# Two-layer hybrid trunk: pair sums in PSUM, weight forms by accumulating DMAs, q, k and v stored in split form

## The chip, the cores and the metric

The kernel runs on one core of a Trainium2 chip. A core has five engines that each work through their own queue in order: TensorE (PE, matrix products into PSUM; its weight loads are shown apart as PEld), VectorE (DVE), ScalarE (ACT), GpSimd (POOL) and SyncE (SP), which here issues nearly all DMAs. The metric is the device time of the whole program in microseconds (us).

## The reference

Two layers, each on 1024 tokens of width 1024, float32:

```python
ada = c_act @ w_ada[l] + b_ada[l]
shift, scale, gate = jnp.split(ada, 3, axis=-1)
h = rmsnorm(x, norm_g[l]) * (1.0 + scale) + shift
p = h @ w_in[l]                       # 1024 x 9224
mq, mk, mv, mo, mz, mi, mf, rq, rk, rv, rz = split_cols(p)
qk = silu(causal_dwconv(concat([mq, mk]), conv_w[l], conv_b[l]))
cell = mlstm_chunkwise(mq_c, mk_c, mv, mi + b_igate[l], mf + b_fgate[l])      # 4 heads x 256
y_m = sigmoid(mo) * head_layernorm(cell, gn_m[l]) * silu(mz)
ret = retention_chunkwise(rotary(rq), rotary(rk), rv)                         # 4 heads x 256
y_r = head_layernorm(ret, gn_r[l]) * silu(rz)
x = x + gate * (concat([y_m, y_r]) @ w_out[l])
```

At the end stands one more RMSNorm. Both kinds of head are causal attention with decay, computed block by block with a running state of 256 x 256: a block's scores (q times k, masked and scaled), the values (scores times v, plus q times the state), and the update of the state (k scaled, times v).

## The kernel before

**Precision.** Each matrix operand is split into a high part of type float32r and a low part, the rest (split_to, L741: ACT writes the high part, POOL or DVE subtracts it from the source). A product is three matmuls (mm3, L149): high x high, high x low, low x high.

**Products in pairs.** The projection p is made by pairs of 128-column tiles (for v: pairs of heads). For two column tiles and two halves of the tokens, eight block products are replaced by seven on sums of blocks (Strassen's way). build_forms (L560) makes the sums of h once a layer; weight_forms (L589) makes those of the weights for every pair: four raw blocks of 128 x 512 come from HBM, four sums are formed in place (on POOL for q and k, on DVE for gates and v, L597 to L603), and seven splits follow (ACT and POOL). pair_units (L659) takes one weight form after the other, in the order of ORDER (L587), and issues 12 matmuls with it into one of the PSUM banks X, Y, Z; combine (L642) copies partial sums to SBUF tiles "acc" (ACT, L646) and adds the next bank to them (DVE, L649); done(...) gets a finished tile of 128 x 512, in SBUF but for the last one, which stays in its bank X. For v, vpair_units (L671) does the same with 48 matmuls of 256 columns per form, one set of banks from each of the PSUM pools pp and pa (four banks each). The Feeder (L629) makes weight forms four ahead (AHEAD); the tiles wH and wL have five buffers each (NW), raw has four.

**After a product.** A z or o tile goes through a gate (L532, L537) and is stored in DRAM (gdr). A q or k tile goes through a short convolution (conv_silu, L745) or a rotation (rot_done, L817), and spill (L795) stores it in DRAM as float32 (qdr, kfr), k also transposed (kdr, L762). v is stored as it is (vdr).

**Attention** of a head (L844) is a generator that is launched when its k is done. It is advanced between products: each unit of a pair is one tick, and "yield n" means that the next piece comes n ticks later. fetch_qk (L852) loads a block of q and k and splits it; fetch_kv (L862) loads v, scales and splits it (v_split, L722), and loads and splits the transposed k (k_rows, L770). A block takes four steps:

```python
for j in range(NCH):
    scores(j + 1); dm_load(j + 2); fetch_kv(j + 1)
    yield 1
    values(j, ...)            # whole blocks: and yield 1
    update(...)               # of the state; dm_make(j + 2)
    yield 1                   # divided blocks (j = 1, 2): values, update of their second half, yield 1
    fetch_qk(j + 2); finish(j)
    yield 1
```

**Order.** The order on PE is the program's own (manual schedule); those of ACT, DVE, POOL and SP are set by a scheduler, which also waits for free buffers. In a layer, v of all eight heads comes first, then for each head q, k and a pair of gates; then the output product (OutLoads L1074, out_units L1104). norm, gate_chain (L443) and rotary_tables (L383) stand around these.

Of the kernel before, what the change touches and what calls it, by code (L numbers as in the profile page):

```python
# [19 lines left out]
P = 128  # L20
# [16 lines left out]
NB = 60  # L37
NACC = 8
NTH = 4
NW = 5  # L40
AHEAD = 4
# [16 lines left out]
N_CONST = 17  # L58


def shape_constants():
    c = np.zeros((P, N_CONST), np.float32)
    step = np.arange(128, dtype=np.float32) * (np.float32(1.0) / np.float32(127.0))
    c[:, C_FREQ] = np.float32(1.0) / (10000.0 ** step.astype(np.float64)).astype(np.float32)
    p = np.arange(P, dtype=np.float64)
    for h in range(NH):
        for tt in range(2):
            c[:, C_GS + 2 * h + tt] = GAMMA[h] ** (-(p + 128 * tt))
            c[:, C_EPS + 2 * h + tt] = EPS * 256.0 * GAMMA[h] ** (-2.0 * (p + 128 * tt))
    return c  # L70
# [15 lines left out]
def tile_hybrid_trunk(ctx, tc, x, xt, c, positions, w_ada, b_ada, norm_g, w_in, conv_w, conv_b,  # L86
# [89 lines left out]
    qdr, kfr = ([[[dpool.tile([HD, HALF], F32, name=f"{n}{l}_{h}_{i}") for i in range(2)] for h in range(8)]  # L176
                 for l in range(DEPTH)] for n in ("qdr", "kfr"))
    vdr = [[[dpool.tile([HALF, HD], F32, name=f"vdr{l}_{h}_{i}") for i in range(2)] for h in range(8)]
           for l in range(DEPTH)]
    mdr = [dpool.tile([NH, T], F32, name=f"mdr{l}") for l in range(DEPTH)]  # L180

# [29 lines left out]
    def head_cols(l, rb):  # L211
# [4 lines left out]
        V.tensor_copy(cl[:, 8:88], pt[:, 0:80])  # L216
        V.tensor_scalar(cl[:, 88:96], pt[:, 80:88], 0.25, None, ALU.mult)
        V.tensor_scalar(cl[:, 96:104], pt[:, 88:96], 0.5, None, ALU.mult)
# [128 lines left out]
    def load_w_raw(src, c0, n):  # L347
        kk = 512 // n
        raws = []
        for p in range(KT // kk):  # L350
            raw = wt("raw", 512, 4)
            Q.dma_start(raw.rearrange("p (a b) -> p a b", a=kk),
                        src[p * kk * P:(p + 1) * kk * P, c0:c0 + n].rearrange("(a p) b -> p a b", p=P))
            raws.append(raw)
            yield raw

    def split_w(raw, n, eng=G, other=False):
        wH, wL = (wt(t, 512, b, F32R) for t, b in ((("acc", NACC),) * 2 if other else (("wH", NW), ("wL", NW))))
        split_to((wH, wL), raw, eng)
        return [(wH[:, a * n:(a + 1) * n], wL[:, a * n:(a + 1) * n]) for a in range(512 // n)]  # L360

    def load_w(src, c0, n):
        res = []
        for raw in load_w_raw(src, c0, n):
            res += split_w(raw, n)
        return res
# [16 lines left out]
    def rotary_tables():  # L383
# [5 lines left out]
        for n in range(4):  # L389
# [6 lines left out]
            yield 1  # L396
            V.tensor_tensor(a2, ang, a1, ALU.subtract)
            V.tensor_scalar(turn, a1, c3, None, ALU.mult)
            yield 1
            V.scalar_tensor_tensor(turn, a2, c3, turn, ALU.mult, ALU.add)  # L400
            V.scalar_tensor_tensor(turn, a2, c2, turn, ALU.mult, ALU.add)
            yield 1
# [17 lines left out]
            yield 2  # L420
# [22 lines left out]
    def gate_chain(l, pgs, gt):  # L443
# [6 lines left out]
        mxs = wt("q", 1024, 2)  # L450
        for half in range(2):
            pg = pgs[half]
            fb, li, e = wt("v", 516, 4)[:, 0:512], wt("v", 516, 4)[:, 0:512], wt("dm", 512, 2)
# [57 lines left out]
        eH, eL = wt("eH", 64, 1, F32R), wt("eL", 64, 1, F32R)  # L511
        A.copy(eH, eul)
        V.tensor_tensor(eL, eul, f(eH), ALU.subtract)
# [16 lines left out]
        gt.update(C4=C4, eul4=eul4, eH=eH, eL=eL, em3=em3, wi=wi, we=we, dc=dc)  # L530

    def gate_z(src, g):  # L532
        th = wt("th", 512, NTH)
        A.activation(th, src, AF.Tanh, scale=0.5)
        V.scalar_tensor_tensor(g, th, 1.0, src, ALU.add, ALU.mult)

    def gate_o(src, g, store):  # L537
        th = wt("th", 512, NTH)
        A.activation(th, src, AF.Tanh, scale=0.5)
# [20 lines left out]
    def build_forms(hT):  # L560
        F = {"11": [hT[k][0] for k in range(4)], "21": [hT[k][0] for k in range(4, 8)],
             "22": [hT[k][1] for k in range(4, 8)], "T1": [], "T2": [], "T3": [], "T4": []}
# [11 lines left out]
        for k in range(4):  # L574
            t1, b12, b22 = whole(hT[k][0]), whole(hT[k][1]), whole(hT[k + 4][1])
            V.tensor_tensor(t1, b12, t1, ALU.subtract)
            V.tensor_tensor(b12, b22, b12, ALU.subtract)
            V.tensor_tensor(b22, b22, t1, ALU.subtract)
            keep("T2", b22)
            keep("T1", t1)  # L580
            keep("T3", b12)
            t4 = whole(hT[k + 4][0])
            V.tensor_tensor(t4, t4, b22, ALU.subtract)
            keep("T4", t4)
        return F

    ORDER = (("X", "11"), ("Y", "21"), ("X", "T2"), ("Z", "T1"), ("X", "T3"), ("Z", "22"), ("X", "T4"))  # L587

    def weight_forms(r11, r12, r21, r22, eng):  # L589
        def split(r):  # L590
            w = (wt("wH", 512, NW, F32R), wt("wL", 512, NW, F32R))
            split_to(w, r)
            return w

        yield split(r11)
        yield split(r12)
        eng.tensor_tensor(r21, r21, r22, ALU.add)  # L597
        eng.tensor_tensor(r11, r21, r11, ALU.subtract)  # L598
        yield split(r11)
        yield split(r21)  # L600
        eng.tensor_tensor(r21, r22, r11, ALU.subtract)
        yield split(r21)
        eng.tensor_tensor(r12, r12, r11, ALU.subtract)  # L603
        yield split(r12)
        yield split(r22)

    def pair_forms(l, cols2, eng):
        raws = {}
        for i, kh in ((0, 0), (0, 1), (1, 0), (1, 1)):
            raw = raws[i, kh] = wt("raw", 512, 4)  # L610
            Q.dma_start(raw.rearrange("p (a b) -> p a b", a=4),
                        w_in[l, kh * 512:(kh + 1) * 512, cols2[i]:cols2[i] + P].rearrange("(a p) b -> p a b", p=P))
        for w in weight_forms(raws[0, 0], raws[0, 1], raws[1, 0], raws[1, 1], eng):
            yield [(w[0][:, k * P:(k + 1) * P], w[1][:, k * P:(k + 1) * P]) for k in range(4)]

    def vpair_forms(l, cols2, eng):
        gens = []
        for kp in range(2):
            raws = {}
            for i, kh in ((0, 0), (0, 1), (1, 0), (1, 1)):  # L620
                raw = raws[i, kh] = bt() if kp else wt("raw", 512, 4)
                r0 = kh * 512 + kp * 256
                Q.dma_start(raw.rearrange("p (a b) -> p a b", a=2),
                            w_in[l, r0:r0 + 256, cols2[i]:cols2[i] + HD].rearrange("(a p) b -> p a b", p=P))
            gens.append(weight_forms(raws[0, 0], raws[0, 1], raws[1, 0], raws[1, 1], eng))
# [16 lines left out]
    def combine(n, bank, keep, done):  # L642
        with tc.high_priority():
            if n in (0, 2, 3):
                keep[n] = wt("acc", 512, NACC)
                A.copy(keep[n], bank["Z" if n == 3 else "X"])  # L646
            elif n < 6:
                b, m = {1: ("Y", 0), 4: ("X", 3), 5: ("Z", 2)}[n]
                V.tensor_tensor(keep[m], bank[b], keep[m], ALU.add)  # L649
        if n == 1:  # L650
            done(0, 0, keep[0])
        elif n == 4:
            done(1, 1, keep[3])
        elif n == 5:
            done(0, 1, keep[2])
        elif n == 6:
            done(1, 0, bank["X"])

    def pair_units(feed, F, done):  # L659
        bank, keep = {}, {}  # L660
        for n, (b, form) in enumerate(ORDER):
# [6 lines left out]
            combine(n, bank, keep, done)  # L668
            yield

    def vpair_units(l, feed, F, heads):  # L671
        banks, keeps = [{}, {}], [{}, {}]

        def stored(part):
            def done(i, half, src):
                if i == 1 and half == 0:
                    t = wt("acc", 512, NACC)
                    A.copy(t, src)
# [844 lines left out]
```

## Time and profile before

| | |
|---|---|
| time, median of 3 runs | 2886.41 us (2884.13 to 2889.84) |
| the profiled execution | 2891.24 us, of which the span of the trace is 2889.5 us |
| mean granted clock of TensorE | 0.893 |
| bytes read from HBM, written | 251.90 MB, 105.94 MB |
| longest total wait on TensorE's queue, one line | 126.2 us (L896 for POOL's split of q) |

The profile gives each engine's busy time and, for groups of equal instructions, count, busy time, mean duration of one, the idle time of the engine before them and what ended it. Lines are those of the kernel printed above; since split_to and mm3 are helpers, many groups have the lines L742, L743 and L150 to L152, and are told apart by their tiles ("wL<-raw,wH" is the low part of a weight form, "q<-acc,q" that of a fetched q). Windows are counted from the start of the span. PEclk is the clock granted to TensorE as a share of the full one.

### The profile page before, as it was taken

Reading aid. Unit: us, or ns where it says so; the run is one execution under the profiler, and the core shown is the slowest. Engines: PE = TensorE matmul, PEld = TensorE weight load, DVE = VectorE, ACT = ScalarE, POOL = GpSimd, SP = SyncE. Lnnn points to the kernel's source line nnn. Section 1 sums busy time; section 2 is a strip of 40 time slices with the busy share of each in tenths; the row PEclk is TensorE's granted clock in tenths of the full one; section 3 lists DMA queues with packets and bytes.
Section 4 is the critical chain, followed back from the end, with each engine's and each line's share of the span. In section 5 each row is a group of like instructions: output and inputs, shape, how many; then the busy total and the mean of one; then the engine's idle time right before and its main releaser. Section 6 shows DMA issues by size and latency. Waiting matters only on the chain. (4 is left out here: it accounts for less than half of the span.)

```text
span 2889.5 us, 35104 instructions
## 1 busy us (share of the span) xinstructions
PE 2302.5 (80%) x11483; PEld 1943.4 (67%) x11483; DVE 1826.2 (63%) x3199; ACT 1163.1 (40%) x2149; POOL 1367.5 (47%) x1098
## 2 busy tenths in 40 slices
PE   4789977777676777789996999788777676767998
PEld 3589966556565556668785998666666555656777
DVE  4994356557566777877527534567567677777744
ACT  4523333333344444454345333333334444444433
POOL 0444664544545545452266446655554545544123
PEclk9899989789788888889998999899888788888999
DMA  7034344433443334347641433444343433424766
GB/s 221 25 85 123 95 118 130 117 120 107 122 123 110 114 105 129 94 132 256 220 142 33 107 99 113 121 120 118 98 127 91 111 109 110 129 82 128 234 195 173
DMA packets 483012, 360.20 MB, mean 125 GB/s; under 512 B 186866, under 2 KB 403706, under 8 KB 482828
## 3 DMA queue, kind: packets, MB, share of 16 engines
q1 hardware_dynamic: 482684, 357.70, 42.5%
q8 instruction: 90, 1.47, 0.2%
q14 instruction: 94, 0.77, 0.1%
q10 hardware_dynamic: 144, 0.26, 0.0%
HBM read 251.90 MB, written 105.94 MB: 124 GB/s over the span
## 5 line engine op out<-in xcount | busy, mean ns | idle before, releaser
L743 POOL TENSOR_TENSOR wL<-raw,wH 128x512 fp32r<-128x512 f32 x492 | 674.4, 1378 | 710.8 <-ACT wH L742 655.9
L150 PE MATMUL pp<-b,wH 128*128 128x512 f32 x1616 | 673.7, 417 | 41.6 <-ACT acc L646 36.7
L151 PE MATMUL pp<-b,wH 128*128 128x512 f32 x1616 | 664.1, 411 | 4.2 <-DVE b L1095 4.2
L152 PE MATMUL pp<-b,wL 128*128 128x512 f32 x1616 | 659.8, 408 | 0.0
L742 ACT CAST wH<-raw 128x512 fp32r<-128x512 f32 x556 | 340.4, 618 | 633.3 <-PE pp L151 269.8
L150 PEld LDWEIGHTS pp<-b,wH 128*128 128x128 f32 x1616 | 331.1, 205 | 116.3 <-ACT acc L646 43.9
L151 PEld LDWEIGHTS pp<-b,wH 128*128 128x128 f32 x1616 | 328.6, 203 | 68.9 <-DVE b L1095 5.8
L152 PEld LDWEIGHTS pp<-b,wL 128*128 128x128 f32 x1616 | 324.1, 201 | 73.8
L896 PE MATMUL pa<-q,kc 128*128 128x256 f32 x384 | 105.5, 423 | 169.5 <-POOL q L743 126.2
L150 PE MATMUL pp<-wH,b 128*128 128x256 f32 (+1 forms) x576 | 182.7, 317 | 57.4 <-ACT wH L742 44.4
L649 DVE TENSOR_TENSOR acc<-pp,acc 128x512 f32<-128x512 f32 x180 | 122.4, 681 | 149.6 <-PE pp L152 137.3
L896 PEld LDWEIGHTS pa<-q,kc 128*128 128x128 f32 x384 | 85.0, 306 | 191.3 <-POOL q L743 139.6
L151 PE MATMUL pp<-wL,b 128*128 128x256 f32 (+1 forms) x576 | 182.0, 316 | 13.2 <-POOL wL L743 13.2
L152 PE MATMUL pp<-wH,b 128*128 128x256 f32 (+1 forms) x576 | 181.4, 315 | 0.2
L150 PE MATMUL pa<-wH,b 128*128 128x256 f32 (+1 forms) x576 | 177.1, 307 | 0.0
L151 PE MATMUL pa<-wL,b 128*128 128x256 f32 (+1 forms) x576 | 176.8, 307 | 0.0
L152 PE MATMUL pa<-wH,b 128*128 128x256 f32 (+1 forms) x576 | 176.6, 307 | 0.0
L150 PEld LDWEIGHTS pp<-wH,b 128*128 128x128 f32 x576 | 113.9, 198 | 65.6 <-ACT wH L742 45.4
L754 DVE SCALAR_TENSOR_TENSOR acc<-acc,cols,acc 128x511 f32<-128x511 f32 x144 | 140.3, 974 | 27.2 <-ACT acc L749 26.1
L743 POOL TENSOR_TENSOR wL<-b,wH 128x512 fp32r<-128x512 f32 x56 | 77.3, 1381 | 159.3 <-ACT wH L742 120.4
L646 ACT COPY acc<-pp 128x512 f32<-128x512 f32 x180 | 104.2, 579 | 111.8 <-PE pp L152 106.7
L151 PEld LDWEIGHTS pp<-wL,b 128*128 128x128 f32 x576 | 114.0, 198 | 20.4 <-POOL wL L743 15.2
(348 smaller groups left out, 4954.2 us busy)
## 6 DMA issues: line engine op xcount, KB each, us to landing
raw<-in_w_in_dram SPq DMA_DIRECT2D x250, 256.0 KB
raw<-in_w_out_dram SPq DMA_DIRECT2D x128, 256.0 KB
gdr<-acc SPq DMA_DIRECT2D x64, 256.0 KB
vdr<-acc SPq DMA_DIRECT2D x64, 256.0 KB
qdr<-acc SPq DMA_DIRECT2D x64, 256.0 KB
kfr<-acc SPq DMA_DIRECT2D x64, 256.0 KB
acc<-qdr SPq DMA_DIRECT2D x64, 256.0 KB
acc<-kfr SPq DMA_DIRECT2D x64, 256.0 KB
```

The costliest lines, as they stand in the source:

```text
L150: PE.matmul(o, lt[0], rt[0], start=start, stop=False, skip_group_check=more)
L151: PE.matmul(o, lt[0], rt[1], start=False, stop=False, skip_group_check=more)
L152: PE.matmul(o, lt[1], rt[0], start=False, stop=stop, skip_group_check=more)
L646: A.copy(keep[n], bank["Z" if n == 3 else "X"])
L649: V.tensor_tensor(keep[m], bank[b], keep[m], ALU.add)
L742: A.copy(dst[0], src)
L743: eng.tensor_tensor(dst[1], src, f(dst[0]), ALU.subtract)
L754: V.scalar_tensor_tensor(acc[:, d:], pt[:, 0:HALF - d], wcol, acc[:, d:], ALU.mult, ALU.add)
L896: PE.matmul(pd, piece(kx[j], i, dt, tt * P, P), qd, start=dt == 0 and i == 0, stop=dt == 1 and i == 1)
```

## The change

- Weights are read from two further inputs, w_blk and w_val, which hold the columns of w_in block by block, so that a row of a raw tile is 2 KB in one piece; before, it was four pieces of 512 B (two of 1 KB for v). q, k, gates and v take 3 plain loads (SP) and 7 loads from POOL's queue for a set of seven forms, where there were 4 plain loads.
- weight_forms: of the seven splits three have their low part on POOL, two on DVE; two ("loaded") are made by a DMA that writes the float32r tile, ACT that writes its negative into wL, and a DMA that adds the float32 block to it. Three of the four sums of blocks are accumulating DMAs, one is on DVE.
- pair_units adds into PSUM: the sums are written to the bank itself (or to a fresh bank of pp), and done(...) gets PSUM tiles; with "loose" (rotary heads) the first one stays in SBUF. The signs of the sums change, so that tiles of the second column come negated; gates, columns and rotations take that sign up. vpair_units keeps both parts in pp, splits v and stores both parts.
- spill splits q and k and stores high and low parts; k's transposed store comes first. Attention loads them ready. v's scale moves to the scores (a factor per key) and to the weights of the transposed k; v lands in two ring tiles whose last column is set once.
- A block of attention has five steps.
- The order of the jobs is given by a string for each layer: in layer 0, v of heads 2 and 3 comes among the heads; in layer 1, v of six heads.
- NACC 8 to 6, NB 60 to 61, raw five buffers instead of four. The third projection before the pairs has its split weights in the q tiles; rotary_tables yields less often.

```diff
-    def weight_forms(r11, r12, r21, r22, eng):
-        def split(r):
-            w = (wt("wH", 512, NW, F32R), wt("wL", 512, NW, F32R))
-            split_to(w, r)
...
-        yield split(r11)
-        yield split(r12)
-        eng.tensor_tensor(r21, r21, r22, ALU.add)
-        eng.tensor_tensor(r11, r21, r11, ALU.subtract)
-        yield split(r11)
...
+    def weight_forms(blk, first):
...
+        def loaded(src):
+            w = tiles()
+            G.dma_start(w[0], src)
+            A.activation(w[1], f(w[0]), AF.Copy, scale=-1.0)
+            G.dma_start(w[1], src, accum_op=ALU.add)
+            return w
+
+        a, s1, s3 = raw(blk[0][0]), raw(blk[1][0]), raw(blk[0][0])
+        G.dma_start(s1, blk[1][1], accum_op=ALU.add)
+        if first == "21":
+            yield loaded(blk[0][1])
+        w = split(a, G)
+        V.tensor_tensor(a, a, s1, ALU.add)
+        yield w
+        if first == "11":
+            yield loaded(blk[0][1])
+        w = split(a, V)
+        G.dma_start(a, blk[0][1], accum_op=ALU.add)
+        G.dma_start(s3, blk[1][0], accum_op=ALU.add)
+        yield w
+        yield split(s1, G)
+        yield split(s3, V)
+        yield split(a, G)
+        yield loaded(blk[1][1])
...
-    def pair_units(feed, F, done):
+    def pair_units(feed, F, done, loose=False):
...
-            combine(n, bank, keep, done)
+            with tc.high_priority():
+                if n in (0, 2, 3):
+                    keep[n] = wt("acc", 512, NACC)
+                    A.copy(keep[n], bank["Z" if n == 3 else "X"])
+                elif n == 1:
+                    c = keep[0] if loose else bank["Y"]
+                    V.tensor_tensor(c, bank["Y"], keep[0], ALU.add)
+                    done(0, 0, c)
+                elif n == 4:
+                    c = ps_p()
+                    V.tensor_tensor(c, bank["X"], keep[3], ALU.add)
+                    done(1, 1, c)
+                elif n == 5:
+                    V.tensor_tensor(bank["Z"], bank["Z"], keep[2], ALU.add)
+                    done(0, 1, bank["Z"])
+                else:
+                    done(1, 0, bank["X"])
             yield
...
+        def store(part, i, half, src):
+            vH, vL = (wt("acc", 512, NACC, F32R) for _ in range(2))
+            A.activation(vH, src, AF.Copy, scale=-1.0 if i else 1.0)
+            if i:
+                V.scalar_tensor_tensor(vL, src, -1.0, f(vH), ALU.mult, ALU.subtract)
+            else:
+                V.tensor_tensor(vL, src, f(vH), ALU.subtract)
...
-                    bank[b] = ps_a() if part else ps_p()
+                    bank[b] = ps_p()
...
     def spill(src, l, hg, which, m, half):
-        dst = (kfr if which else qdr)[l][hg][half]
-        Q.dma_start(dst[m * P:(m + 1) * P, :], src)
+        dst = (kfr if which else qdr)[l][hg][half].rearrange("(a p) t -> a p t", p=P)
         if which:
             k_store(src, l, hg, m, half)
+        hi, lo = wt("acc", 512, NACC, F32R), src.bitcast(F32R)
+        split_to((hi, lo), src)
+        Q.dma_start(dst[m], f(hi))
+        Q.dma_start(dst[2 + m], src)
...
+        def load_qk(dst, dr, tag, bufs, j):
+            if j < NCH:
                 t = dst[j] = wt(tag, 1024, bufs, F32R)
-                split_to((t[:, 0:512], t[:, 512:1024]), a)
...
+                Q.dma_start(f(t).rearrange("p (a t) -> p a t", a=4),
+                            dr[l][hg][j // 2].rearrange("(a p) t -> p a t", p=P)[:, :, (j % 2) * CH:(j % 2 + 1) * CH])
...
+        def load_v(j):
+            if j < NCH:
+                r = ring3[taken[0] % 2]
+                taken[0] += 1
+                Q.dma_start(f(r[:, :, 0:HD]), vdr[l][hg][j].rearrange("(a p) c -> p a c", p=P))
+                vs[j] = (r[:, 0:2], r[:, 2:4])
...
-                V.tensor_tensor(sd[:, 0:CH], ps[:, 0:CH], dmat[:, 0:CH], ALU.mult)
...
+                V.scalar_tensor_tensor(sd[:, 0:CH], ps[:, 0:CH], sc[0], dmat[:, 0:CH], ALU.mult, ALU.mult)
...
         for j in range(NCH):
             whole = j in WHOLE
+            values(j, (0, 1) if whole else (0,))
+            if j < NCH - 1:
+                update((2 * j, 2 * j + 1) if whole else (2 * j,))
+            yield 1
             if j + 1 < NCH:
                 scores(j + 1)
+                load_k(j + 2)
                 dm_load(j + 2)
-            fetch_kv(j + 1)
-            yield 1
-            values(j, (0, 1) if whole else (0,))
-            if whole:
-                yield 1
-            if j < NCH - 1:
-                update((2 * j, 2 * j + 1) if whole else (2 * j,))
-            dm_make(j + 2)
-            yield 1
+            load_kt(j + 1)
+            yield 2
             if not whole:
                 values(j, (1,))
                 update((2 * j + 1,))
-                yield 1
-            fetch_qk(j + 2)
+            dm_make(j + 2)
+            load_q(j + 2)
+            load_v(j + 2)
             finish(j)
-            yield 1
+            yield 2
...
-        vh = ((4, 5), (6, 7), (0, 1), (2, 3))
-        heads = (4, 5, 6, 7, 0, 1, 2, 3)
...
+        plan = ("v45 v67 v01 q4 k4 z4 q5 k5 z5 q6 k6 z6 q7 k7 z7 q0 k0 a10 a11 q1 k1 v23 q2 k2 a20 q3 k3 a21 a30 a31",
+                "v45 q4 k4 z4 q5 k5 v67 q6 k6 z5 z6 q7 k7 v01 q0 k0 z7 a10 q1 k1 v23 q2 k2 a11 a20 q3 k3 a21 a30 a31")[l]
```

401 lines of the change are left out of this document (188 added, 213 removed).

## The prediction

> **What bounds the kernel now.** I read the page first for the shares of the engines.
>
> ```profile
> PE 2302.5 (80%) x11483; PEld 1943.4 (67%) x11483; DVE 1826.2 (63%) x3199; ACT 1163.1 (40%) x2149; POOL 1367.5 (47%) x1098
> q1 hardware_dynamic: 482684, 357.70, 42.5%
> ```
>
> No engine is full; TensorE comes nearest. Where it loses time shows in a table by stretches: the two attention stages (355 to 1297 and 1770 to 2697 us), and two stretches that run without a hole.
>
> ```profile
> core 0: us, PE busy (x) PEld busy (x) DVE busy (x) ACT busy (x) POOL busy (x), PEclk, DMA share, GB/s
> 250.00:300.00 50.00, 50.00 (x419) 50.00 (x418) 15.27 (x18) 16.90 (x29) 23.41 (x18) 1.00 0.33 100
> 355.00:1297.00 942.00, 700.50 (x3138) 578.58 (x3137) 631.48 (x1170) 369.94 (x713) 474.20 (x391) 0.85 0.41 118
> 1200.00:1250.00 50.00, 42.64 (x216) 35.31 (x214) 41.59 (x85) 25.39 (x48) 25.21 (x21) 1.00 0.40 114
> 1350.00:1390.00 40.00, 40.00 (x179) 33.10 (x178) 19.12 (x21) 15.24 (x25) 23.56 (x18) 1.00 0.79 256
> 1770.00:2697.00 927.00, 710.61 (x3213) 587.23 (x3212) 641.51 (x1176) 382.54 (x737) 481.23 (x399) 0.87 0.41 115
> ```
>
> The dense stretches give the price of a matmul: 50.00/419 = 119 ns with 256 columns, 40.00/179 = 223 ns with 512. A stage has 26 pairs of 84 matmuls with 512 columns, 2184 in all; the rest (3138 - 2184 = 954, and 3213 - 2184 = 1029) are attention's. Dense, the stages would take 2184 x 0.223 + 954 x 0.119 = 601 us and 610 us, 1211 together, where they take 942 + 927 = 1869. Of the 658 us lost, (942 - 700.5) + (927 - 710.6) = 458 are idle; the other 200 are matmuls at a lowered clock (0.85 and 0.87). So one us of idle costs 658/458 = 1.43 us here. (From 1200 to 1250 us 7.4 idle us cost no clock at all; hence 1.43 is an average, and 1.0 its lower end.)
>
> Who makes TensorE wait is in the list of waits:
>
> ```profile
> POOL wL L743 <- ACT wH L742: 786.2, 275, 30.8
> ...
> PE pa L896 <- POOL q L743: 126.2, 32, 7.7
> PE pa L150 <- ACT kc L742: 123.1, 22, 10.3
> ...
> PE pa L976 <- ACT cH L742: 59.0, 13, 8.0
> ...
> PE pa L896 <- POOL kc L743: 43.3, 32, 3.0
> ...
> PE pp L150 <- ACT acc L646: 38.7, 17, 8.8
> ...
> PE pa L152 <- POOL kc L743: 33.3, 26, 3.0
> ...
> PE pa L151 <- POOL q L743: 17.6, 18, 3.1
> ```
>
> Nearly all of it is attention waiting for its own q and k: the scores (L896, and mm3 at L150 to L152) wait until ScalarE and GpSimd have split the fetched blocks. The chain that ended last runs through one such place; the columns are start, length and what:
>
> ```profile
> 1950.35 1.69 POOL raw L598
> ...
> 1953.68 1.71 POOL q L743
> 1955.39 1.68 POOL kc L743
> ...
> 1957.11 1.87 PE pa L896 x7
> ```
>
> GpSimd is not full but in order: the split stands behind a weight sum, and fetch_qk comes only one step ahead of the scores.
>
> **The change, part by part.**
>
> 1. q and k are split once, when stored (spill), and fetched ready. The waits on kc and q go: 126.2 + 123.1 + 43.3 + 33.3 + 17.6 = 343.5 us, x 1.43 = **-491**. Late next is the fetch itself: q is asked for three steps ahead of its scores and k five, and a step holds 12 matmuls (2.7 us), so 8 us or more against a landing of 2.6 to 4.2 (rows below); I cost it at nothing. If that cover goes, a late landing costs its lateness 64 times. The 128 splits stay on POOL, in spill; the first scores of a head stand seven steps (19 us) behind the last product, against a conv, a split, a store and a fetch of some 14 us.
>
> 2. Five steps a block instead of four. Between update and the values that read the new state stand five steps in a whole block (before: three), three and two in a divided one (before: one and three). Of the 59.0 us on cH I take half, with 0 and 59 as ends: 29.5 x 1.43 = **-42**.
>
> 3. The v split leaves attention, pair sums go to PSUM, 140 weight splits go from POOL to DVE.
>
> ```profile
> L734 DVE SCALAR_TENSOR_TENSOR v<-acc,kc,v 128x256 fp32r<-128x256 f32 x64 | 51.7, 838 | 36.5 <-ACT v L733 36.5
> ...
> L743 DVE TENSOR_TENSOR wL<-raw,wH 128x512 fp32r<-128x512 f32 x64 | 43.5, 685 | 12.3 <-ACT wH L742 10.8 <-DMA raw<-in_w_out_dram 1.0
> L734 DVE SCALAR_TENSOR_TENSOR v<-acc,eul,v 128x256 fp32r<-128x256 f32 x64 | 42.6, 685 | 14.0 <-ACT v L733 13.8
> ...
> L754 DVE SCALAR_TENSOR_TENSOR acc<-acc,cols,acc 128x511 f32<-128x511 f32 x48 | 41.6, 867 | 26.5 <-ACT acc L749 26.1
> ...
> L827 DVE TENSOR_TENSOR th<-acc,dm 128x512 f32<-128x512 f32 x16 | 27.2, 1700 | 0.0
> ...
> L597 DVE TENSOR_TENSOR raw<-raw,raw 128x512 f32<-128x512 f32 x28 | 24.2, 863 | 36.1 <-DMA raw<-in_w_in_dram 34.7 <-issue 1.4
> ...
> L754 DVE SCALAR_TENSOR_TENSOR acc<-pp,cols,acc 128x511 f32<-128x511 f32 x16 | 11.7, 734 | 0.0
> ...
> L827 DVE TENSOR_TENSOR th<-pp,dm 128x512 f32<-128x512 f32 x16 | 10.8, 674 | 0.0
> ```
>
> The same operation is shorter from PSUM: 734 against 867, 674 against 1700. DVE by counts of the built order: v splits -51.7 - 42.6; 144 conv steps x 0.133 = -19; 16 x 1.026 = -16; 76 weight sums fewer x 0.863 = -66; 140 splits x 0.685 = +96; 64 splits of v at the store x 0.685 = +44. That is -55 in 1826: off the path, but no relief either, 1220 of the stages' 631 + 642. The price is in the banks: pair_units now keeps up to four pp banks until DVE has read them, where SBUF copies freed them. Today's wait for a copied bank (38.7 us) is the nearest row; I add 50 us (ends 0 and 120), x 1.43 = **+72**.
>
> 4. Weight sums and two of seven splits by DMAs from POOL's queue.
>
> ```profile
> L743 POOL TENSOR_TENSOR wL<-raw,wH 128x512 fp32r<-128x512 f32 x492 | 674.4, 1378 | 710.8 <-ACT wH L742 655.9 <-PE pp L152 32.8 <-PE pp L151 13.3
> ...
> L597 POOL TENSOR_TENSOR raw<-raw,raw 128x512 f32<-128x512 f32 x32 | 45.5, 1422 | 26.2 <-DMA raw<-in_w_in_dram 26.2
> ```
>
> POOL loses 272 splits x 1.378 = 375 us and 128 sums x 1.422 = 182 us, and gets 476 DMA issues. No issue on POOL is in this trace. Its price lies between SP's (0.41) and a whole POOL operation (1.38); I take the middle, 0.9, no row being nearer: 428 us, so POOL falls from 1367 to some 1240 (ends 1005 and 1467).
>
> ```profile
> L611 SPq DMA_DIRECT2D raw<-in_w_in_dram x208: 367/411/1127, 299.9 to 2633.5; - x104
> ```
>
> What counts is the new chain of a loaded form: when its wH tile is free, POOL issues the load, it lands, ScalarE writes the negative, POOL issues the accumulation, it lands. Landings of 256 KB on the chain that ended last:
>
> ```profile
> 1905.01 3.20 DMA raw<-in_w_in_dram
> ...
> 2437.76 2.81 DMA acc<-qdr
> ...
> 2796.35 5.11 DMA raw<-in_w_out_dram
> ```
>
> The DMA engines get busier (below), so I take 4.2, between 3.2 and 5.1. With ScalarE's 0.62 (the wH cast) and one POOL operation queued ahead of each issue (1.4), the chain is 0.62 + 2 x (0.9 + 4.2 + 1.4) = 13.6 us. Its cover is four forms: 4 x 12 x 0.223 = 10.7 us, 13.2 with attention's share between (601/487 of it), 12.0 in the middle. A late form also lengthens the cover of the next, so half of the 1.6 us is left: 0.8 x 136 forms (two for each of 52 pairs and 16 v sets) = 109 us, x 1.43 = **+156**. Behind POOL's wait stand the wL and sL splits, behind ScalarE's the sH cast and the evacuations. With an issue of 0.41 it is +62, with 1.38 +251.
>
> ```profile
> L742 ACT CAST wH<-raw 128x512 fp32r<-128x512 f32 x556 | 340.4, 618 | 633.3 <-PE pp L151 269.8 <-POOL raw L601 83.8 <-POOL raw L598 68.8
> ```
>
> The Trainium skill ("DMA: Bandwidth & Descriptors", section "Anatomy of one DMA — SWDGE (gpsimd) path") fits such a DMA as 2.0 us plus bytes over 436e3 per us, by my estimate 2.6 us for 256 KB. By it the chain is 10.4 us, nothing is late and the sum is 156 us lower; no DMA of that path is in this trace.
>
> 5. The rest I cost at nothing: TensorE's count is unchanged in the built order (11428); the v pairs moved between attention's steps (layer 1) cost the same dense time; raw loads in rows of 2 KB only lighten SP's transfers; SP issues 1951 rather than 1827, 124 x 0.41 = 51 us of a queue that is mostly waiting; NACC 8 to 6 and NRAW 4 to 5 touch stages that are over 93% dense.
>
> Sum against the profiled execution (span 2889.5, time 2891.2): 2891 - 491 - 42 + 72 + 156 = 2586. The median shown lies 4.8 lower, so **2580 us**.
>
> **The rivals.**
>
> *Clean.* Nothing takes the waits' place: 2891 - 491 - 42 - 5 = 2353, up to 2480. For it: the skill's shorter landing. Against it: DVE at 1220 us in stages that would shrink to 1336.
>
> *The DMA engines fill up.* A stage moves 118 GB/s x 0.942 ms = 111 MB. Added are 6 transfers for each of 26 pairs and 160 for q, k and v, 83 MB; five accumulations a pair also read their target, 34 MB: 228 MB. At 256/0.79 = 324 GB/s that is 704 us of a stage of some 780. Then landings are 5.1, the chain 15.4, each loaded form 1.7 late: +331 instead of +156, 2755.
>
> *POOL's issue is long (slower).* Place: the same chain. At 4.2 us landing it decides from 2.5 us an issue: chain 16.8, 2.4 late x 136 x 1.43 = 467, which with the banks' 72 eats the 533. At 3.5 us the chain is 18.8, 3.4 late, 661 us: 3086. Against it: POOL's dearest row of this size is under 1.5. For it, as a mechanism: L827 at 1700 beside 674 shows POOL and DVE blocking each other when both of DVE's inputs are in SBUF. The Trainium skill ("SBUF — State Buffer", section "SBUF: two separate sides") says of software DMAs that DVE's two-port copies lock GpSimd out of writing descriptors, 620 ns becoming 3100; such copies are rare here, and no row shows it.
>
> **How the numbers follow.** Forecast 0.58 (its own range 2480 to 2680, by the ends of the issue price), clean 0.10, DMA engines 0.20, long issue 0.12. About 0.2% is what a measurement of this kernel can tell from no change; 0.01, out of the DMA case's tail, is left for it. Faster 0.87, same 0.01, slower 0.12. The range 2400 to 2810 leaves out the slower case and the clean one's lower half.
>
> **What would show it.** The waits of L896 and mm3 on kc and q gone, clock above 0.9 in the stages: step 1. Waits of mm3 on an accumulating DMA or on the negated tile: step 4, with POOL's issue durations as its price. Waits on a pp bank: step 3. A DMA share above 0.8: the second rival. Wrong would be: q or k landing late, or POOL's issues above 2.5 us.

## The result and the profile after

The changed kernel takes 2915.54 us (median of 3 runs, 2911.5 to 2921.4) against 2886.41 before: 1.0102 times as long, 95% interval 1.007 to 1.0134. The forecast was 2580 us. The profiled execution has a span of 2909.8 us.

The page of the changed kernel, its engines and its DMA queues (packets, MB, share of 16 engines):

```profile
PE 2279.8 (78%) x11483; PEld 1931.8 (66%) x11483; DVE 1677.8 (58%) x3073; ACT 1142.9 (39%) x2091; POOL 1151.3 (40%) x1174
q1 hardware_dynamic: 463676, 440.55, 48.3%
q0 software_dynamic: 68544, 124.81, 24.0%
```

VectorE and GpSimd lost the work that was meant to go (1826 to 1678, 1367 to 1151), and TensorE still idles more than before: 2909.8 - 2279.8 = 630 us, where 2889.5 - 2302.5 = 587 were lost. In the table by stretches (columns as before the change: window, PE, PEld, DVE, ACT, POOL busy, clock, DMA share, GB/s) the v stage and the two attention stages stand; the latter are still thin, at much the same clock (0.88; before 0.85 and 0.87), with the DMA engines near 0.8 where 0.41 stood; and the v stage has more holes. Its row in the kernel before:

```profile
150.00:300.00 150.00, 136.66 (x1080) 134.81 (x1080) 95.09 (x161) 45.77 (x80) 63.82 (x46) 0.95 0.35 98
```

The three stretches in the changed kernel:

```profile
150.00:300.00 150.00, 116.19 (x867) 113.46 (x866) 93.78 (x185) 45.02 (x80) 50.33 (x53) 0.85 0.75 188
350.00:1300.00 950.00, 720.14 (x3516) 604.20 (x3516) 562.20 (x1102) 365.83 (x690) 388.40 (x420) 0.88 0.78 206
1750.00:2700.00 950.00, 735.24 (x3848) 634.67 (x3849) 533.57 (x1038) 369.58 (x697) 390.25 (x427) 0.88 0.77 201
```

From the list of waits of the changed kernel (us in total, times, longest):

```profile
POOL wL L619 <- ACT wL L618: 333.8, 89, 7.7
PE pp L154 <- ACT acc L674: 326.0, 54, 17.7
ACT wL L618 <- DMA wH<-in_w_blk_dram: 288.8, 87, 8.1
ACT wL L618 <- DMA wH<-in_w_val_dram: 107.0, 29, 13.2
PE pp L155 <- DMA wL<-in_w_val_dram: 57.7, 15, 8.1
PE pa L154 <- ACT b L806: 29.8, 13, 4.9
```

The scores' waits for q and kc, 343.5 us before, are down to 24.5 (on the landing of kc). In their place TensorE waits 326.0 us for the copies of X and Z that ScalarE makes between two groups of a pair (L674; the same copy, L646, cost 38.7 before). One such wait, by the timeline of ScalarE and then of TensorE (start, length, what, idle time before it and its releaser):

```profile
801.91 0.77 ACT L766 ACTIVATE acc<-pp,cols 128x512 f32<-128x512 f32 x1
807.81 0.63 ACT L618 ACTIVATE wL<-wH 128x512 fp32r<-128x512 f32 x1 [5.13 <-DMA wH<-in_w_blk_dram]
808.35 0.61 ACT L775 ACTIVATE th<-acc 128x512 f32<-128x512 f32 x1
809.72 0.62 ACT L759 CAST acc<-acc 128x512 fp32r<-128x512 f32 x1 [0.76 <-DVE acc L776]
810.25 0.77 ACT L766 ACTIVATE acc<-pp,cols 128x512 f32<-128x512 f32 x1
813.60 0.63 ACT L775 ACTIVATE th<-acc 128x512 f32<-128x512 f32 x1 [2.58 <-DVE acc L773]
814.98 0.62 ACT L759 CAST acc<-acc 128x512 fp32r<-128x512 f32 x1 [0.76 <-DMA ndr<-zt]
815.51 0.58 ACT L674 COPY acc<-pp 128x512 f32<-128x512 f32 x1
```

```profile
816.14 0.79 PE L154 MATMUL pp<-b,wH 128*128 128x512 f32 x1 [15.12 <-ACT acc L674]
```

The copy is 0.58 us of work, and it stands last in a queue of two convolutions of the pair before (L766, tanh L775, cast of the stored split L759) and one negative that waits 5.13 us for its load to land. ScalarE is 39% busy, and TensorE waits 15 us for it.

Three theories came from this, and the expectations below use their names: **late loads** (the negatives' waits keep the copies back), **store chains** (the stored split's chain does), **full DMA engines**. With them went the forecast's own step 3, the banks.

### The profile page after: what moved, and what is told of

Read it like the earlier page. It is cut to its first block, busy times and chain, and to the rows that moved or that the text cites. A ratio compares the mean times of both kernels' runs of the same rounds, so it can differ in the third digit from the quotient of the medians.

```text
span 2909.8 us, 35824 instructions
## 1 busy us (share of the span) xinstructions
PE 2279.8 (78%) x11483; PEld 1931.8 (66%) x11483; DVE 1677.8 (58%) x3073; ACT 1142.9 (39%) x2091; POOL 1151.3 (40%) x1174
## 5 line engine op out<-in xcount | busy, mean ns | idle before, releaser
L154 PE MATMUL pp<-b,wH 128*128 128x512 f32 x1616 | 681.6, 422 | 338.1 <-ACT acc L674 326.0
L760 POOL TENSOR_TENSOR wL<-raw,wH 128x512 fp32r<-128x512 f32 x276 | 392.0, 1433 | 405.4 <-ACT wH L759 332.2
L759 ACT CAST wH<-raw 128x512 fp32r<-128x512 f32 x476 | 289.7, 616 | 372.0 <-PE pp L155 129.8
L155 PE MATMUL pp<-wL,b 128*128 128x256 f32 (+1 forms) x1024 | 325.2, 318 | 64.5 <-DMA wL<-in_w_val_dram 57.7
L154 PE MATMUL pp<-wH,b 128*128 128x256 f32 (+1 forms) x1024 | 325.7, 318 | 55.4 <-ACT acc L720 24.5
L156 PE MATMUL pp<-wH,b 128*128 128x256 f32 (+1 forms) x1024 | 321.8, 314 | 0.2
L155 PEld LDWEIGHTS pp<-wL,b 128*128 128x128 f32 x1024 | 215.3, 210 | 74.3 <-DMA wL<-in_w_val_dram 61.0
L154 PEld LDWEIGHTS pp<-wH,b 128*128 128x128 f32 x1024 | 215.0, 210 | 66.6 <-ACT acc L720 25.8
L618 ACT ACTIVATE wL<-wH 128x512 fp32r<-128x512 f32 x136 | 85.7, 630 | 430.2 <-DMA wH<-in_w_blk_dram 288.8
L760 POOL TENSOR_TENSOR acc<-acc,acc 128x512 fp32r<-128x512 f32 x128 | 179.7, 1420 | 156.4 <-ACT acc L759 126.0
L619 POOL DMA_DIRECT2D wL<-in_w_blk_dram x104 | 92.0, 884 | 343.1 <-ACT wL L618 260.4
L760 DVE TENSOR_TENSOR wL<-raw,wH 128x512 fp32r<-128x512 f32 x200 | 156.7, 785 | 111.6 <-ACT wH L759 111.1
L156 PEld LDWEIGHTS pp<-wH,b 128*128 128x128 f32 x1024 | 214.9, 210 | 7.3 <-DVE b L1120 2.4
L771 DVE SCALAR_TENSOR_TENSOR acc<-pp,cols,acc 128x511 f32<-128x511 f32 (+2 forms) x192 | 142.4, 742 | 33.4 <-ACT acc L766 32.1
L759 ACT CAST acc<-acc 128x512 fp32r<-128x512 f32 x128 | 78.4, 617 | 130.7 <-DVE acc L848 48.3
```

The costliest lines, as they stand in the source:

```text
L154: PE.matmul(o, lt[0], rt[0], start=start, stop=False, skip_group_check=more)
L155: PE.matmul(o, lt[0], rt[1], start=False, stop=False, skip_group_check=more)
L156: PE.matmul(o, lt[1], rt[0], start=False, stop=stop, skip_group_check=more)
L618: A.activation(w[1], f(w[0]), AF.Copy, scale=-1.0)
L619: G.dma_start(w[1], src, accum_op=ALU.add)
L759: A.copy(dst[0], src)
```

## The experiments

Times are medians. The kernel before took 2889.7 to 2893.0 us beside these runs; ratios are to it, with their 95% interval.

**e1_plain_loaded.** The changed kernel, the two loaded splits made ordinary:

```diff
-            w = tiles()
-            G.dma_start(w[0], src)
-            A.activation(w[1], f(w[0]), AF.Copy, scale=-1.0)
-            G.dma_start(w[1], src, accum_op=ALU.add)
-            return w
+            t = bt() if first == "21" else wt("raw", 512, NRAW)
+            Q.dma_start(t, src)
+            return split(t, G)
```

> The changed kernel (2915.5 us) with one part undone: the two loaded splits of a set of seven (cast load, negative on ScalarE, accumulating load) are ordinary splits again, of a block that SP fetches; the accumulated sums stay. Theory 'late loads': ScalarE stands 396 us before its negatives, waiting for a load to land, and the copies of X and Z that TensorE waits 326 us for stand behind them; with the direct waits of mm3 on the accumulated tile (66 us) some 120 us of TensorE's idle time go, x 1.43 = 170: 2745 us. Theory 'store chains' (the copies stand behind the conv, tanh and split of the pair before, in ScalarE's order and for want of acc tiles): the waits on the copy stay above 250 us, 2870 to 2930. Theory 'full DMA engines': 136 transfers of 256 KB and their re-reads fewer of some 950, 2850.

Measured 2805.3 us (0.9711, 0.9688 to 0.9735). The loaded splits cost 110 us. The edit takes out their lateness, and with it 36 MB of transfers (567.9 to 532.2 MB). TensorE's wait for the copies only fell from 326 to 280 us: the negatives are not what keeps most of those.

**e2_engine_sums_and_splits.** The sums too: four raw blocks, four sums on the engines.

```diff
+        a, b, s1, d = raw(blk[0][0]), raw(blk[0][1]), raw(blk[1][0]), raw(blk[1][1])
+        G.tensor_tensor(s1, s1, d, ALU.add)
...
+        G.tensor_tensor(s1, a, d, ALU.subtract)
+        V.tensor_tensor(b, a, b, ALU.add)
```

> The changed kernel with all weight forms made as before the change: four blocks fetched by SP, four sums on GpSimd and VectorE, seven splits; nothing accumulates by DMA, GpSimd issues none. Attention, the stored splits and the pair sums in PSUM stay. 'Late loads': as in the run with ordinary splits or better, 2700 to 2750. 'Full DMA engines': the traffic falls from 568 to some 480 MB, landings from 5 to 3.5 us, 2650 to 2750. 'Store chains': within 2% of 2915, the waits on the copy of X and Z above 250 us, since ScalarE's order and the acc tiles are untouched; GpSimd gets some 290 + 190 us of work back and may cost 50 us.

Measured 2739.6 us (0.9484, 0.9463 to 0.9504), another 66 us less, with another 71 MB fewer (460.9 MB). All of step 4 so costs 2915.5 - 2739.6 = 176 us, and without it the change would be a gain of 150. The copies stay the first wait:

```profile
PE pp L154 <- ACT acc L666: 265.5, 44, 16.8
PE pp L154 <- ACT wH L751: 65.4, 9, 22.1
```

**e3_eight_acc.** `NACC = 6` to `NACC = 8` in the changed kernel, paid for with one big tile (`NB = 61` to `60`) and the sharing of two small tags.

> The changed kernel with eight acc tiles in place of six, as before the change (paid for with one big tile and the sharing of two small tags). 'Store chains' for want of acc tiles: the copies and the conv starts no longer wait for the stores of the pair before to land; of the 326 us before copies at least half go, x 1.43: 2650 to 2700. 'Late loads' and 'full DMA engines': within 1% of 2915. If only ScalarE's order counts and not the tiles: 2860 to 2915.

Measured 2936.2 us (1.0165, 1.014 to 1.0191), slower than the changed kernel by 21: more tiles in the common pool, at that price, are no help.

**e4_sums_in_sbuf.** The changed kernel, its pair sums back in SBUF (`c = keep[0]`, `c = keep[3]`, and Z's sum into `keep[2]`).

> The changed kernel with the pair sums written to the SBUF copies as before the change, so that the banks Y, Z and the fourth one come free at the sum. 'Banks' (my step 3: TensorE and the copies wait because VectorE and ScalarE still read a bank): the waits before the first product of a pair shrink by half, 2750 to 2800. 'Want of acc tiles': the sums hold acc tiles longer, 2920 to 3000. 'Late loads': within 1% of 2915.

Measured 2951.4 us (1.0214, 1.0197 to 1.0231): 36 us slower, in the range of 'want of acc tiles'. Sums in PSUM are a gain here; whether by the banks or by the acc tiles that the other form holds longer, this run can't tell.

**e5_before_stored_split.** The kernel before, with the stored form of step 1 alone. The lead, that is how long before its scores a block is asked for, stays at one step:

```diff
-        dst = (kfr if which else qdr)[l][hg][half]
-        Q.dma_start(dst[m * P:(m + 1) * P, :], src)
+        hi, lo = wt("acc", 512, NACC, F32R), src.bitcast(F32R)
+        split_to((hi, lo), src)
+        Q.dma_start(dst[m], f(hi))
+        Q.dma_start(dst[2 + m], src)
```

> The kernel before (2889.7 us) with my step 1 alone: q and k are split when stored and fetched ready; everything else as before. Theory 'the wait moves into the pairs' (ScalarE does its work in order; the split's cast now waits there for the conv or the rotation, and the copies of X and Z that TensorE needs stand behind it): the waits on kc and q go, waits of mm3 on the copy rise from 39 us to some 200, and the time is 2700 to 2800. Theory 'step 1 is right, other parts of the change eat it' (order of steps, pair sums, v): 2400 to 2480, copies still under 60 us.

Measured 2864.6 us (0.9907, 0.9891 to 0.9924), 27 us less, where step 1 (with the longer lead) had said -491; both theories had the time far lower. From its list of waits on TensorE:

```profile
PE pp L150 <- ACT acc L646: 328.1, 42, 18.1
PE pa L897 <- DMA kc<-kfr: 61.7, 15, 9.2
PE pa L150 <- DMA kc<-kfr: 10.8, 6, 3.3
PE pa L150 <- DMA q<-qdr: 10.2, 4, 3.2
```

The 343.5 us for the splits are gone, and 328.1 us for the copies (38.7 before) and 82.7 for the fetches stand in their place. TensorE's idle time even rose, from 587 to 604 us. This shows most of the forecast's failure in one run: the waits go, the idle time stays.

**e6_cast_on_dve.** e2, with the cast of the stored split on VectorE (`V.tensor_copy(hi, src)`).

> The version with all weight forms on the engines (2739.6 us) with one edit: the cast of the stored split is made by VectorE (tensor_copy), not by ScalarE, so that ScalarE no longer waits for the conv's or the rotation's result at that place. 'The wait moves into the pairs' through the cast: of the 265 us before copies about half go, x 1.43 = 190, less 128 x 0.5 = 64 us of VectorE: 2580 to 2680. If only the conv's own chain (its tanh) or the pair's order counts: 2720 to 2790.

Measured 2732.8 us (0.9447, 0.9433 to 0.9461): 7 us. The one instruction that was added to ScalarE's queue isn't what keeps the copies; they still wait 231.5 us.

**e7_split_at_fetch.** e2 without step 1: plain store, split after the fetch, the longer lead kept.

```diff
+                a = wt("acc", 512, NACC)
+                Q.dma_start(a.rearrange("p (m t) -> p m t", m=2),
+                            dr[l][hg][j // 2]...[:, 0:2, (j % 2) * CH:(j % 2 + 1) * CH])
+                split_to((t[:, 0:512], t[:, 512:1024]), a)
```

> The version with all weight forms on the engines (2739.6 us) with step 1 undone: q and k are stored plain and split when fetched, but asked for three and five steps ahead of the scores as in the changed kernel. 'The wait moves into the pairs': the copies' wait falls below 120 us and the scores wait for q and kc again, though less than 343 us because of the longer lead; the sum lies within 2% of 2740. 'Stored split is a gain as forecast, other parts eat it': some 300 us or more slower, 3000 to 3100.

Measured 2620.9 us (0.9064, 0.9051 to 0.9078). Neither sentence had expected this: taking step 1 out makes the kernel 119 us faster, and the scores hardly wait. From the list of waits on TensorE:

```profile
PE pa L992 <- ACT cH L751: 64.5, 14, 9.4
PE pp L154 <- ACT acc L666: 40.7, 20, 3.8
PE pa L156 <- POOL kc L752: 12.7, 11, 2.5
PE pa L154 <- ACT kc L751: 9.5, 6, 2.8
```

The stored form isn't needed to end the waits for kc and q: 31 us are left of 343.5, all rows together. TensorE idles 2618.8 - 2232.2 = 387 us, where e2 has 2739.4 - 2233.6 = 506 at the same busy time: the 119 us are idle time, all of them.

**e8_done_late.** e2, with the chains (`done(...)`) called outside `tc.high_priority()`, as before the change.

> The version with all weight forms on the engines (2739.6 us) with the conv, rotation and gate chains called outside the high priority again, as before the change, so that a pair's copies may be put ahead of the chain of the pair before in ScalarE's order. 'The order of ScalarE': waits on the copies fall from 265 to some 100 us, 2500 to 2600. 'The chain's length' (the copy waits for its bank or tile whatever the priority): within 1% of 2740.

Measured 2740.4 us (0.9475, 0.9455 to 0.9496): nothing.

**e9_own_tiles.** The changed kernel, with two tiles for the copies alone, paid for as in e3:

```diff
-                    keep[n] = wt("acc", 512, NACC)
+                    keep[n] = wt("keep", 512, 2)
```

> The changed kernel (2915.5 us) with one edit: a pair's copies of X and Z get two tiles of their own and take none of the six acc tiles, which the stored splits also fill and which come free only when a store has landed. 'Slots' (the copies stand behind the conv chain in ScalarE's order because no acc tile is free earlier; eight acc tiles did not help because the chains took them too): TensorE's wait on the copies falls from 326 to below 120 us, 2600 to 2720. 'Order by time' (the chain is simply ready first) or 'late loads alone': the wait stays above 250, 2880 to 2930.

Measured 2905.4 us (1.0045, 1.0031 to 1.006), 10 us better. The mechanism was right and its worth was not. The copies did stand behind the chains for want of a tile, and now wait 50 us; but other waits take what they give up. From the list again:

```profile
PE pa L154 <- ACT b L806: 99.0, 25, 9.5
PE pp L155 <- DMA wL<-in_w_val_dram: 71.3, 17, 9.0
PE pp L154 <- ACT keep L674: 50.4, 30, 4.8
PE pp L156 <- DMA wL<-in_w_blk_dram: 36.8, 17, 4.7
PE pa L154 <- DMA kc<-kfr: 31.3, 9, 14.2
```

Of the 276 us taken from the copies 53 are gone from TensorE's idle time (630 to 577), and its busy time rose by 43 (2280 to 2323, the same 11483 matmuls). A wait on one label is what stands last, not what the time is worth.

**e10_after_split_at_fetch.** The changed kernel without step 1 (the edit of e7).

> The changed kernel (2915.5 us) with my step 1 alone undone: q and k stored plain, split when fetched, still three and five steps ahead. The accumulating DMAs stay. 'Slots': as with the weight forms on the engines (there 2739.6 to 2620.9), 2750 to 2820, waits on the copies under 150 us, scores' waits on q and kc under 80. 'Late loads' (with the DMA forms, ScalarE's waits for loads keep the copies late): 2880 to 2930.

Measured 2821.7 us (0.9755, 0.9725 to 0.9784): 94 us, beside the DMA forms. Again it is idle time (630 to 2816.9 - 2280.5 = 536 us), and the copies' wait falls from 326 to 82.

**e11_pairs_on_engines_own_tiles** and **e12_pairs_own_tiles_fetch.** Own tiles as in e9 and the pairs' weight forms as in e2 (v's stay with the DMAs); the second also with the edit of e7.

> The changed kernel with own tiles for the copies, and the weight forms of the pairs (not those of v) made on the engines again. 'Slots': both costs are gone but for v's, 2915 - 330 - 150 = 2480 to 2580. If own tiles do nothing: 2740 to 2780.

> The version before this one (own tiles, pairs' weight forms on the engines) with q and k split at the fetch. With the copies free of the acc tiles, the stored split is judged by itself: if it is worth something, this one is 20 to 60 us slower than that; if its own traffic and tiles still cost, this one is 20 to 80 us faster, 2450 to 2560.

Measured 2746.8 us (0.9498, 0.9478 to 0.9518) and 2654.6 us (0.9179, 0.916 to 0.9198). The theory of the slots, which expected 2480 to 2580 of e11, falls as an account of the time. (No run has this mix of weight forms without own tiles, so what the tiles are worth here stays unmeasured.) The stored split costs 92 us with tiles of their own for the copies, 119 and 94 without: most of its price isn't the copies' tiles.

**e13_fetch_plus_traffic.** e7, with the transfers of the stored form and no more:

```diff
         Q.dma_start(dst[m], src)
+        Q.dma_start(dst[2 + m], src)
...
+                Q.dma_start(f(t)[:, 512:1024].rearrange("p (m t) -> p m t", m=2), ...[:, 2:4, ...])
```

> The version with the weight forms on the engines and q and k split at the fetch (2620.9 us), with the stored split's transfers added and nothing else: each product is stored twice, and each fetch brings as many bytes as the split form has (the second half is overwritten by the split). 'Traffic' (the 67 MB more, and the landings they delay, are what the stored split costs): 2700 to 2740. 'Place' (the split's chain at the end of a pair is what costs): 2615 to 2650.

Measured 2695.3 us (0.9322, 0.9288 to 0.9355), between the two: the transfers and what they hold make 74 of the 119 us, the place of the split the other 45, if the two add up. But this version has a wait that the stored form hasn't: GpSimd writes its low part over the second fetch, and stands until that has landed, 48.8 us in all, none of it in e7:

```profile
POOL kc L752 <- DMA kc<-kfr: 25.9, 11, 11.7
POOL q L752 <- DMA q<-qdr: 22.9, 6, 7.9
```

So the 74 may be too much for the transfers. In the first stage (330 to 1200 us of e7, then of this run) the DMA share goes from 0.49 to 0.56, and the clock falls:

```profile
330.00:1200.00 870.00, 735.98 (x3619) 619.25 (x3619) 621.55 (x1210) 381.38 (x720) 372.09 (x322) 0.92 0.49 150
```

```profile
330.00:1200.00 870.00, 718.20 (x3444) 600.97 (x3443) 590.81 (x1143) 360.06 (x682) 364.70 (x318) 0.89 0.56 177
```

**e14_own_queues.** e2, the high part stored from ScalarE's DMA queue, the low part from GpSimd's (`A.dma_start`, `G.dma_start`).

> The version with the weight forms on the engines and the stored split (2739.6 us), with the two stores of a split issued by the engines that made them (ScalarE's queue for the high part, GpSimd's for the low one), so that SP's queue no longer waits for them. 'SP's queue' (fetches and raw loads stand behind stores that wait 338 us for ScalarE and GpSimd): 2620 to 2680. 'Place' or 'traffic': 2720 to 2800, the issues' own time making it no faster.

Measured 2729.9 us (0.9442, 0.9426 to 0.9457): 10 us. The stores' place in SP's queue is not the cause.

**e15_fetch_done_late.** e7 with the edit of e8.

> The version with the weight forms on the engines and q and k split at the fetch (2620.9 us), with the conv, rotation and gate chains outside the high priority as before the change. If priority counts once the split is gone from the chain: 2560 to 2610. As with the stored split, where it did nothing: within 1% of 2621.

Measured 2606.0 us (0.9011, 0.8991 to 0.903): 15 us, and the fastest version here, 10% under the kernel before.

**e16_fetch_short_lead.** e7, with q and k asked for one step ahead of the scores:

```diff
+            if j > 0:
+                load_q(j + 1)
+                load_k(j + 1)
             values(j, (0, 1) if whole else (0,))
...
-                load_k(j + 2)
...
-            load_q(j + 2)
```

> The version with the weight forms on the engines and q and k split at the fetch (2620.9 us), with q and k asked for one step ahead of the scores, as before the change, in place of three and five. 'The lead removed the waits' (not the stored form): the scores wait for q and kc 250 us or more again, 2850 to 2950. If the waits had another cause: within 2% of 2621.

Measured 2719.4 us (0.9402, 0.938 to 0.9425). The lead is worth 98 us, less than expected; the waits on q and kc come back to 140 us (126 in these rows of the list) and not to 343:

```profile
PE pa L908 <- POOL q L752: 36.9, 9, 6.6
PE pa L154 <- ACT kc L751: 28.4, 14, 3.5
PE pa L156 <- POOL kc L752: 23.8, 21, 3.7
PE pa L908 <- POOL kc L752: 18.8, 15, 2.9
PE pa L155 <- POOL q L752: 18.3, 11, 3.1
```

**e17_before_rows.** The kernel before, its raw blocks read from w_blk and w_val (`Q.dma_start(raw, w_blk[l, ..., kh])`).

> The kernel before (2889.7 us) with the weight blocks of the pairs and of v read from the layout of the changed kernel (2 KB a row in place of 512 B or 1 KB), nothing else. Step 5 as forecast: within 0.5% of 2890. If shorter landings bring the 171 us: 2720 to 2800.

Measured 2888.6 us (0.9983, 0.9971 to 0.9996): 4 us, as step 5 had it.

**e18_splits_on_gpsimd.** e7, with `split(a, V)`, `split(s1, V)` and `split(d, V)` on G.

> The version with the weight forms on the engines and q and k split at the fetch (2620.9 us), with all seven splits of a set on GpSimd as before the change (three of seven were on VectorE, 204 in all, x 1.43 us = 292 us more on GpSimd, 160 less on VectorE). Step 3 as forecast (engines not on the path): 2600 to 2650. If GpSimd's in-order queue was what bound the kernel before: 2700 to 2800.

Measured 2669.7 us (0.9223, 0.9198 to 0.9249): 49 us slower. The 204 splits are worth that on VectorE, though GpSimd would be only 50% busy with them, and VectorE is 76 us busier with them (1777 against 1701).

## Why the prediction was wrong, by its own steps

The steps measured, in a chain of versions that ends at the changed kernel:

| from, to | us | forecast |
|---|---|---|
| before 2890, e16 2719: steps 2, 3, 5 and the rest of attention | -171 | +30 |
| e16, e7 2621: the longer lead of q and k | -98 | in step 1 |
| e7, e2 2740: q and k split at the store | +119 | in step 1: -491 together |
| e2, changed 2915.5: step 4 | +176 | +156 |

**Step 1 failed**: it said that the waits on kc and q, 343.5 us, go and that 491 us of time go with them. The waits went, as the trace shows; the time did not. Lead and stored form together are worth +21 in this chain (the stored form at the old lead, on the kernel before, e5, -27). Of some 335 us by which the forecast missed, step 1 so makes 512, step 4 makes 20, and steps 2, 3 and 5 take 201 back. Two assumptions in step 1 were wrong. First, it put what is late next at nothing, and looked there only at the fetch, the next link of the same chain. The fetch is small indeed, 24.5 us in the changed kernel, though the landings that its cover was held against, "2.6 to 4.2", run from 2.81 to 5.11 in the rows it pointed to. What it missed: the 128 splits were not removed but moved, to the end of the pairs, where ScalarE's casts and the acc tiles stand between TensorE and its next group; the copies of X and Z took over the very wait (38.7 to 328.1 in e5). Second, a sum of waits with one label was taken for time; the prediction called it nearly all of TensorE's loss, and it was 343.5 of 587 us idle. e9 shows what such a sum can be worth: 276 us taken from one label bought 10. The factor 1.43 was not the fault: from before to e7 idle time fell by 587 - 387 = 200 us and the span by 271, a factor of 1.35.

**What in step 1 was right** is the lead: it takes the waits from 140 us (e16) to 31 (e7) and gives 98 us. The first 204 of the 343.5 us had gone without it, to other parts of the change that no run takes apart. The stored form that came with the lead costs more than that gives. Up to 74 of its 119 us come with its transfers (e13), which step 1 did not price; the second rival counted them, but as a matter of full DMA engines, and here the share was 0.56. By which path is open: TensorE itself hardly waits longer for DMAs in e13 (16 us for 12), GpSimd does (237 us for 172, and most of the growth is the wait that only e13 has), the second store also holds its acc tile longer, and the second fetch needs its kc tile earlier. The 45 us of the place are not split further either; the cast on ScalarE (e6), the priority (e8), the copies' tiles (e9) and SP's queue (e14) are each worth 10 us or less.

**Steps 2, 3 and 5** were too dark by 200 us. The banks, +72, are not to be seen. The row on which that term stood, TensorE's wait for a copied bank, is 326 us in the changed kernel for 38.7 before, but 40.7 in e7, which has the pair sums in PSUM too and lacks the stored split and the DMA forms; for VectorE's sum out of a bank (L681) TensorE waits 0.7 us; and putting the sums back costs 36 (e4). That VectorE and GpSimd are off the path is wrong as well: 204 splits moved off GpSimd gain 49 (e18). The rows of 2 KB are nothing, as said (e17). If these gains hold in the chain, some 86 us of the 171 are not taken apart (five steps, v split outside attention, the scores' operations). Step 2 can't be judged by its wait on cH, 59.0 us before: in the changed kernel 2.1 us are left, but TensorE waits for the copies there, and where it doesn't, in e7, the wait is 64.5. No run undoes the five steps alone.

**Step 4** has the right size, 176 for 156, in part by luck: its 156 stood for the loaded forms, which cost 110 us (e1), and the sums by DMA, which it put at nothing, cost the other 66. GpSimd's issues and the landings, on which it stood, are near the forecast's, in the rows of the load (L617) and the accumulation (L619) of a loaded form (ns and us, each min/median/max):

```profile
L617 POOL DMA_DIRECT2D wH<-in_w_blk_dram x104: 554/616/1162, 302.5 to 2689.3; - x104
DMA to landing us min/median/max: 2.8/4.8/8.9
```

```profile
L619 POOL DMA_DIRECT2D wL<-in_w_blk_dram x104: 835/865/1193, 309.1 to 2693.3; - x104
DMA to landing us min/median/max: 3.7/4.6/8.4
```

Issues of 0.62 and 0.87 us for a forecast of 0.9, landings of 4.8 and 4.6 for 4.2. The estimate from the fit in the Trainium skill ("DMA: Bandwidth & Descriptors", section "Anatomy of one DMA — SWDGE (gpsimd) path") was 2.6 us; the shortest of the loads here took 2.8 us. The second rival's 5.1 us for a landing on nearly full DMA engines (a share of 0.78 here) is as near as the forecast's. That lateness makes the price is argued and not shown. ScalarE stands 396 us before its negatives, but TensorE itself waits 57.7 us for the low part of a loaded form of v and 8.0 for one of the pairs, which are 104 of the 136. And the traffic goes with the forms: if a MB cost what it seems to in e13 (74 us for 67 MB, perhaps too much), the 36 MB that e1 takes out would be an estimated 40 of its 110 us, and the 71 MB of e2 all of its 66. No run tells the two apart.

**The slower rival** came true in its sign and not in its mechanism: it asked for issues above 2.5 us, and the longest of the 476 is 1.49 (L623).

## What to carry to other kernels

A wait that is traced to an engine working in order goes to whoever is behind it when the work is moved rather than removed; before it is booked as a gain, ask where the moved instructions will stand and who queues there, and take the sum of a label's waits as an upper bound that can be worth almost nothing. Asking earlier gained 98 us here without a byte more, where the stored second form cost more than that: try the lead first. And an edit that pays and one that costs are often in the same change, so undo them one at a time: here the versions without one or both of the parts that cost were 2 to 10% under the kernel before.

## What the runs showed of the hardware that was not expected

- The version with 67 MB of added transfers (393.7 to 460.9 MB, e13) is 74 us slower with the DMA engines at a share of 0.56 in the first stage, where the changed kernel reaches 0.78; part of it may be GpSimd's wait of 48.8 us for the second fetch. The granted clock in that stage fell from 0.92 to 0.89.
- TensorE's busy time for the same 11483 matmuls lay between 2220 (e14) and 2323 us (e9). Of the 53 us of idle time that e9 saved over the changed kernel 43 came back as busy time of TensorE, though its mean granted clock was higher (0.901 for 0.888); why is not shown.
- GpSimd's shortest issue of an accumulating DMA of 256 KB took 835 ns, that of a plain load of the same size 553. The medians lie apart for loads from w_blk (865 and 616 ns), hardly for those from w_val (867 and 858). Accumulating ones land about as late as plain ones (medians of 4.6 to 5.3 us for 4.8).
